# Three slots of 65024-byte rows with half-row loads, full-row late stores and 4096-column instructions, in an element-wise kernel limited by its transfers

## The chip, the cores and the metric

The kernel runs on one core of a Trainium2 chip. The metric is the device time of one execution in microseconds (us), as a median of several runs. The profile shows compute engines (ACT, DVE, POOL) and 16 DMA engines, which moved 536.98 MB in the kernel before, nearly all of it its input and output, between HBM, the main memory, and the on-chip memory SBUF. PSUM is another on-chip memory. All runs compared here are fast, with a granted clock of 1.0, unless the text says otherwise.

## The reference

The kernel computes the inverse complementary error function of 8192 x 8192 floats. That is 268 MB in and 268 MB out, and every element stands alone.

```python
def setup_inputs():
    return {"x": np.clip(np.random.randn(8192, 8192).astype(np.float32) * 0.3 + 1.0, 0.01, 1.99)}

def reference(x):
    return special.erfcinv(x).astype(np.float32)
```

Both kernels approximate it by `(ln(1 - (x-1)^2) + KAPPA) * (B*x - B)`. Nothing in the argument depends on that formula.

## The kernel before

The input is cut into tiles: 128 partitions, each with one contiguous row of 12288 floats (49152 bytes). Four buffers turn round. The SP queue issues loads, and the ACT queue issues stores. A load into a buffer waits until the store that last read this buffer has landed. Each tile is loaded by one DMA and stored by one DMA, both in full rows.

```python
_FULL = 12288
_HEAD = (2048, 6144)
_TAIL = (6144, 4096, 2048)

_CHUNK = 2048
_BUFS = 4

_LEAD = 49152

# ... (pools, constants)
    io = ctx.enter_context(tc.tile_pool(name="io", bufs=_BUFS))
    psum = ctx.enter_context(
        tc.tile_pool(name="ps", bufs=2, space=bass.MemoryType.PSUM)
    )

    def flat(ap, i):
        return ap[P * starts[i] : P * starts[i + 1]].rearrange("(p w) -> p w", p=P)

    views = []
    room = 0

    def load():
        nonlocal room, buf
        i = len(views)
        w = widths[i]
        if w > room:
            buf, room = io.tile([P, _FULL], fp32, name="xt"), _FULL
        v = buf[:, _FULL - room : _FULL - room + w]
        room -= w
        views.append(v)
        nc.sync.dma_start(out=v, in_=flat(xf, i))

    buf = None

    def compute(i):
        step = min(_CHUNK, widths[i] // 2)
        for c in range(0, widths[i], step):
            d = views[i][:, c : c + step]
            ps = psum.tile([P, _CHUNK], fp32, name="ps")
            s = ps[:, 0:step]
            nc.scalar.activation(
                out=s, in_=d, func=mybir.ActivationFunctionType.Square,
                bias=neg_one, scale=1.0,
            )
            nc.scalar.activation(
                out=s, in_=s, func=mybir.ActivationFunctionType.Ln,
                bias=pos_one, scale=-1.0,
            )
            nc.gpsimd.tensor_scalar(
                out=d, in0=d, scalar1=float(_B), scalar2=float(-_B),
                op0=mult, op1=add,
            )
            nc.vector.scalar_tensor_tensor(
                out=d, in0=s, scalar=float(_KAPPA), in1=d, op0=add, op1=mult
            )

    ctx.enter_context(tc.manual_schedule())
    for i in range(n):
        while len(views) < n and starts[len(views) + 1] - starts[i] <= _LEAD:
            load()
        compute(i)
        nc.scalar.dma_start(out=flat(of, i), in_=views[i])
```

Cuts: the imports, the constants and the launch.

Of the kernel before, what the change touches and what calls it, by code (L numbers as in the profile page):

```python
# [1 line left out]

# [4 lines left out]


_B = 0.24401313
_KAPPA = -3.62385604  # L10



_FULL = 12288
_HEAD = (2048, 6144)
_TAIL = (6144, 4096, 2048)

_CHUNK = 2048
_BUFS = 4

_LEAD = 49152


@with_exitstack
def kernel(
    ctx: ExitStack,
    tc: tile.TileContext,
    x: bass.AP,
    out: bass.AP,
):  # L30
    nc = tc.nc
    P = nc.NUM_PARTITIONS
    fp32 = mybir.dt.float32
    mult = mybir.AluOpType.mult
    add = mybir.AluOpType.add

    xf = x.rearrange("r c -> (r c)")
    of = out.rearrange("r c -> (r c)")
    cols = x.shape[0] * x.shape[1] // P
    n_full, rest = divmod(cols - sum(_HEAD) - sum(_TAIL), _FULL)  # L40
    assert rest == 0
    widths = list(_HEAD) + [_FULL] * n_full + list(_TAIL)
    n = len(widths)
    starts = [0]
    for w in widths:
        starts.append(starts[-1] + w)

    consts = ctx.enter_context(tc.tile_pool(name="consts", bufs=1))
    neg_one = consts.tile([P, 1], fp32)
    nc.vector.memset(neg_one, -1.0)  # L50
    pos_one = consts.tile([P, 1], fp32)
    nc.vector.memset(pos_one, 1.0)  # L52

    io = ctx.enter_context(tc.tile_pool(name="io", bufs=_BUFS))
    psum = ctx.enter_context(
        tc.tile_pool(name="ps", bufs=2, space=bass.MemoryType.PSUM)
    )

    def flat(ap, i):
        return ap[P * starts[i] : P * starts[i + 1]].rearrange("(p w) -> p w", p=P)  # L60

    views = []
    room = 0

    def load():
        nonlocal room, buf
        i = len(views)
        w = widths[i]
        if w > room:
            buf, room = io.tile([P, _FULL], fp32, name="xt"), _FULL  # L70
        v = buf[:, _FULL - room : _FULL - room + w]
        room -= w
        views.append(v)
        nc.sync.dma_start(out=v, in_=flat(xf, i))  # L74

    buf = None

    def compute(i):
        step = min(_CHUNK, widths[i] // 2)
        for c in range(0, widths[i], step):  # L80
            d = views[i][:, c : c + step]
            ps = psum.tile([P, _CHUNK], fp32, name="ps")
            s = ps[:, 0:step]
            nc.scalar.activation(  # L84
                out=s, in_=d, func=mybir.ActivationFunctionType.Square,
                bias=neg_one, scale=1.0,
            )
            nc.scalar.activation(  # L88
                out=s, in_=s, func=mybir.ActivationFunctionType.Ln,
                bias=pos_one, scale=-1.0,  # L90
            )
            nc.gpsimd.tensor_scalar(  # L92
                out=d, in0=d, scalar1=float(_B), scalar2=float(-_B),
                op0=mult, op1=add,
            )
            nc.vector.scalar_tensor_tensor(  # L96
                out=d, in0=s, scalar=float(_KAPPA), in1=d, op0=add, op1=mult
            )

    ctx.enter_context(tc.manual_schedule())  # L100
    for i in range(n):
        while len(views) < n and starts[len(views) + 1] - starts[i] <= _LEAD:
            load()
        compute(i)
        nc.scalar.dma_start(out=flat(of, i), in_=views[i])  # L105


# [1 line left out]
_INS = ['x']  # L109
_OUTS = [((8192, 8192), 'float32')]  # L110


# [23 lines left out]
```

## Time and profile before

| what | value |
|---|---|
| median of 3 runs | 1249.54 us (1247.71 to 1253.46) |
| span of the profiled run | 1245.9 us |
| bytes moved | 536.98 MB at 431 GB/s |
| busy: ACT, DVE, POOL | 79%, 47%, 39% |

These lines are from the page of the kernel before. The line DMA is the busy share of the 16 DMA engines in 40 equal slices of the span, in tenths; GB/s is what they moved. q1 is the load queue, q10 the store queue. The line after those gives the shares of the chain of work that ended last. The last two give the DMA issues: count, size of each, and the median time from issue to landing.

```profile
span 1245.9 us, 1637 instructions
DMA  9999999999999999999999999999999999999998
GB/s 393 431 432 437 439 432 431 429 436 439 436 431 429 436 431 443 429 431 431 437 441 431 431 431 437 429 440 431 433 432 434 441 431 431 431 437 434 431 429 371
DMA packets 13261, 536.98 MB, mean 431 GB/s; under 512 B 1472, under 2 KB 1472, under 8 KB 1472
q1 hardware_dynamic: 6624, 268.44, 49.9%
q10 hardware_dynamic: 6624, 268.44, 49.8%
...
DMA 74%; ACT 22%; DVE 3%; issue 0%; another core or an unknown queue 0%; SPq 0%; ACTq 0%; DVEq 0%
...
xt<-in_x_dram SPq DMA_DIRECT2D x41, 6144.0 KB, 45.9
out_dram<-xt ACTq DMA_DIRECT2D x41, 6144.0 KB, 44.5
```

From the view of waits: who waited for whom, the total in us, how often, and the longest wait. The first line is ACT waiting for loaded data, the second the load queue waiting for a buffer.

```profile
ACT ps L84 <- DMA xt<-in_x_dram: 224.4, 40, 6.7
```

```profile
SPq L74 <- DMA out_dram<-xt: 1145.7, 40, 33.1
```

From the groups of instructions with shapes kept apart (busy us, mean ns of one | idle before it and its releaser), the two sizes of one ACTIVATE.

```profile
L84 ACT ACTIVATE ps<-xt,neg_one 128x2048 f32<-128x2048 f32 x254 | 499.1, 1965 | 232.8 <-DMA xt<-in_x_dram 219.8 <-DVE xt L96 13.0
...
L84 ACT ACTIVATE ps<-xt,neg_one 128x1024 f32<-128x1024 f32 x4 | 4.5, 1114 | 4.6 <-DMA xt<-in_x_dram 4.6
```

From the table by stretches (stretch, length, busy time of DVE, ACT and POOL, clock, DMA share, GB/s): nearly the whole run, and a piece from its middle.

```profile
2.00:1236.00 1234.00, 584.60 (x256) 984.47 (x516) 484.86 (x256) 1.00 1.00 433
500.00:620.00 120.00, 57.50 (x26) 96.28 (x51) 47.52 (x25) 1.00 1.00 433
```

The trace also has one record for each DMA packet, with start, duration and size. One row is one packet (41 DMAs of 128 rows are 5248 packets of 49152 bytes in each queue), and each DMA ends in 16 more packets of 4 bytes (1472 for 92 DMAs, about 9 ns each). The records of this kernel give 611 ns for 16384 bytes, 912 for 24576 and 1815 for 49152. So a packet takes 36.74 ns per 1000 bytes and about 9 ns more: 27.2 GB/s per engine, 435 GB/s for 16.

### The profile page before, as it was taken

How to read it: one execution, taken by the hardware profiler on the slowest of the kernel's cores; microseconds unless marked ns; L12 is line 12 of the kernel's file. 1: busy time of each engine (PE TensorE's matmuls, PEld its weight loads, DVE VectorE, ACT ScalarE, POOL GpSimd, SP SyncE). 2: the span in 40 equal slices, each digit the busy share in tenths (PEclk: the TensorE clock that was granted, in tenths of full speed). 3: DMA queues.
4: the chain of work that ended last, by engine and by line, in shares of the span. 5: the costliest groups of instructions: out<-in, count | busy, mean ns of one | idle time of the engine just before them, and what ended most of it. 6: DMA issues, size and time to landing. Idle time of an engine off the chain costs nothing.

```text
span 1245.9 us, 1637 instructions
## 1 busy us (share of the span) xinstructions
DVE 587.1 (47%) x260; ACT 987.7 (79%) x518; POOL 487.2 (39%) x262
## 2 busy tenths in 40 slices
DVE  3555545444444444444454444544444444444453
ACT  6999887778887788888877788888888878777895
POOL 2444443333433344343433334343343434333342
DMA  9999999999999999999999999999999999999998
GB/s 393 431 432 437 439 432 431 429 436 439 436 431 429 436 431 443 429 431 431 437 441 431 431 431 437 429 440 431 433 432 434 441 431 431 431 437 434 431 429 371
DMA packets 13261, 536.98 MB, mean 431 GB/s; under 512 B 1472, under 2 KB 1472, under 8 KB 1472
## 3 DMA queue, kind: packets, MB, share of 16 engines
q1 hardware_dynamic: 6624, 268.44, 49.9%
q10 hardware_dynamic: 6624, 268.44, 49.8%
q14 instruction: 13, 0.11, 0.0%
HBM read 268.44 MB, written 268.44 MB: 431 GB/s over the span
## 4 chain that ended last, share of the span: by engine, by line
DMA 74%; ACT 22%; DVE 3%; issue 0%; another core or an unknown queue 0%; SPq 0%; ACTq 0%; DVEq 0%
DMA xt<-in_x_dram 39%; DMA out_dram<-xt 35%; ACT ps L88 11%; ACT ps L84 11%; DVE xt L96 3%; SPq L74 0%; ACTq L105 0%; DVEq L96 0%
## 5 line engine op out<-in xcount | busy, mean ns | idle before, releaser
L96 DVE SCALAR_TENSOR_TENSOR xt<-ps,xt 128x2048 f32<-128x2048 f32 (+1 forms) x258 | 587.0, 2275 | 652.6 <-POOL xt L92 642.9
L92 POOL TENSOR_SCALAR xt<-xt 128x2048 f32<-128x2048 f32 (+1 forms) x258 | 487.0, 1887 | 751.8 <-ACT ps L84 749.9
L84 ACT ACTIVATE ps<-xt,neg_one 128x2048 f32<-128x2048 f32 (+1 forms) x258 | 503.6, 1952 | 237.5 <-DMA xt<-in_x_dram 224.4
L88 ACT ACTIVATE ps<-ps,pos_one 128x2048 f32<-128x2048 f32 (+1 forms) x258 | 497.6, 1929 | 8.4
L84 ACT ACT_TABLE_LOAD x1 | 1.3, 1283 | 5.7 <-DMA xt<-in_x_dram 5.7
L88 ACT ACT_TABLE_LOAD x1 | 1.3, 1283 | 0.0
L50 DVE MEMSET neg_one<- 128x1 f32 x1 | 0.1, 59 | 0.8 <-PEq L120 0.8
L120 POOL MEMSET const-float32-0.0<- 128x1 f32 x1 | 0.1, 99 | 0.2 <-issue 0.2
L120 POOL MEMSET const-bfloat16-1.0<- 128x1 bf16 x1 | 0.1, 102 | 0.0
L120 POOL MEMSET const-uint8-127<- 128x1 uint8 x1 | 0.1, 102 | 0.0
L120 POOL MEMSET const-float32-1.0<- 128x1 f32 x1 | 0.1, 99 | 0.0
L52 DVE MEMSET pos_one<- 128x1 f32 x1 | 0.1, 59 | 0.0
## 6 DMA issues: line engine op xcount, KB each, us to landing
xt<-in_x_dram SPq DMA_DIRECT2D x41, 6144.0 KB, 45.9
out_dram<-xt ACTq DMA_DIRECT2D x41, 6144.0 KB, 44.5
xt<-in_x_dram SPq DMA_DIRECT2D x2, 3072.0 KB, 25.4
out_dram<-xt ACTq DMA_DIRECT2D x2, 3072.0 KB, 23.1
xt<-in_x_dram SPq DMA_DIRECT2D x2, 1024.0 KB, 37.4
out_dram<-xt ACTq DMA_DIRECT2D x2, 1024.0 KB, 13.3
xt<-in_x_dram SPq DMA_DIRECT2D x1, 2048.0 KB, 58.0
out_dram<-xt ACTq DMA_DIRECT2D x1, 2048.0 KB, 9.8
```

The source lines that it names most:

```text
L50: nc.vector.memset(neg_one, -1.0)
L52: nc.vector.memset(pos_one, 1.0)
L84: nc.scalar.activation(out=s, in_=d, func=mybir.ActivationFunctionType.Square, bias=neg_one, scale=1.0,)
L88: nc.scalar.activation(out=s, in_=s, func=mybir.ActivationFunctionType.Ln, bias=pos_one, scale=-1.0,)
L92: nc.gpsimd.tensor_scalar(out=d, in0=d, scalar1=float(_B), scalar2=float(-_B), op0=mult, op1=add,)
L96: nc.vector.scalar_tensor_tensor(out=d, in0=s, scalar=float(_KAPPA), in1=d, op0=add, op1=mult)
L120: nc = _bacc.Bacc("TRN2", target_bir_lowering=False, num_devices=1)
```

## The change

The intent is to use longer rows and longer instructions. Three slots of 16256 columns (65024 bytes) take the place of four of 12288. A slot is loaded in two half rows (8192 and 8064 columns) so that computing can start early, and stored in one full row. The store is issued one pair of ACT instructions late, so that ACT never waits for DVE before it issues. Instructions have up to 4096 columns; their intermediate results alternate between PSUM and an SBUF buffer. The ends of the run are cut differently. The core of the diff:

```diff
-_FULL = 12288
-_HEAD = (2048, 6144)
-_TAIL = (6144, 4096, 2048)
 
-_CHUNK = 2048
-_BUFS = 4
+_SLOT = 16256
+_BUFS = 3
 
-_LEAD = 49152
+
+_FULL = ((8192, 8064), (4032, 4096, 4032, 4096), ((16256, 1),))
+
+_HEAD = ((2048, 6144, 4032), (1024, 1024, 2048, 4032, 4096), ((8128, 1), (4096, 1)))
+
+_LAST = (
+    (_FULL[0], _FULL[1], ((16256, 4),)),
+    _FULL,
+    ((4096, 4032), (2048, 2048, 2048, 1008, 976), ((6144, 1), (1984, 1))),
+)
 # ... cut: sums of the slots ...
+    temp = ctx.enter_context(tc.tile_pool(name="temp", bufs=1))
+    temps = ((psum, 4096), (temp, 4032))
 # ... cut: compute() is the same four instructions, into temps in turn ...
     def load():
+        i = len(bufs)
+        b = io.tile([P, _SLOT], fp32, name="xt")
+        bufs.append(b)
+        a = 0
+        for w in slots[i][0]:
+            nc.sync.dma_start(out=b[:, a : a + w], in_=rows(xf, i)[:, a : a + w])
+            a += w
 # ...
+    def store(i, a, w, pieces):
+        nc.scalar.dma_start(
+            out=rows(of, i)[:, a : a + w], in_=bufs[i][:, a : a + w],
+            max_dma_last_dim=None if pieces == 1 else w * 4 // pieces,
+        )
 # ...
+    def issue():
+        while due:
+            i, a, w, pieces = due.pop(0)
+            store(i, a, w, pieces)
+            if a + w == sum(slots[i][0]) and len(bufs) < n:
+                load()
+
     for i in range(n):
-        while len(views) < n and starts[len(views) + 1] - starts[i] <= _LEAD:
-            load()
-        compute(i)
-        nc.scalar.dma_start(out=flat(of, i), in_=views[i])
+        loads, chunks, stores = slots[i]
+        a = done = k = 0
+        for c in chunks:
+            compute(bufs[i][:, a : a + c])
+            issue()
+            a += c
+            while k < len(stores) and done + stores[k][0] <= a:
+                due.append((i, done) + stores[k])
+                done += stores[k][0]
+                k += 1
+    issue()
```

A slot is written as `(loads, instruction widths, stores)`, and a store as `(columns, packets per row)`.

More of the change, by code (lines that the diff above doesn't have):

```diff
@@ L39 @@
     cols = x.shape[0] * x.shape[1] // P
-    n_full, rest = divmod(cols - sum(_HEAD) - sum(_TAIL), _FULL)
+    ends = sum(sum(s[0]) for s in (_HEAD,) + _LAST)
+    n_full, rest = divmod(cols - ends, sum(_FULL[0]))
     assert rest == 0
-    widths = list(_HEAD) + [_FULL] * n_full + list(_TAIL)
-    n = len(widths)
-    starts = [0]
-    for w in widths:
-        starts.append(starts[-1] + w)
+    slots = [_HEAD] + [_FULL] * n_full + list(_LAST)
+    n = len(slots)
+    base = [0]
+    for loads, chunks, stores in slots:
+        w = sum(loads)
+        assert w == sum(chunks) == sum(s for s, _ in stores) and w <= _SLOT
+        base.append(base[-1] + w)
     consts = ctx.enter_context(tc.tile_pool(name="consts", bufs=1))
@@ L55 @@
     psum = ctx.enter_context(
-        tc.tile_pool(name="ps", bufs=2, space=bass.MemoryType.PSUM)
+        tc.tile_pool(name="ps", bufs=1, space=bass.MemoryType.PSUM)
     )
-    def flat(ap, i):
-        return ap[P * starts[i] : P * starts[i + 1]].rearrange("(p w) -> p w", p=P)
-    views = []
-    room = 0
-    def load():
-        nonlocal room, buf
-        i = len(views)
-        w = widths[i]
-        if w > room:
-            buf, room = io.tile([P, _FULL], fp32, name="xt"), _FULL
-        v = buf[:, _FULL - room : _FULL - room + w]
-        room -= w
-        views.append(v)
-        nc.sync.dma_start(out=v, in_=flat(xf, i))
@@ L76 @@
-    buf = None
-    def compute(i):
-        step = min(_CHUNK, widths[i] // 2)
-        for c in range(0, widths[i], step):
-            d = views[i][:, c : c + step]
-            ps = psum.tile([P, _CHUNK], fp32, name="ps")
-            s = ps[:, 0:step]
-            nc.scalar.activation(
-                out=s, in_=d, func=mybir.ActivationFunctionType.Square,
-                bias=neg_one, scale=1.0,
-            )
-            nc.scalar.activation(
-                out=s, in_=s, func=mybir.ActivationFunctionType.Ln,
-                bias=pos_one, scale=-1.0,
-            )
-            nc.gpsimd.tensor_scalar(
-                out=d, in0=d, scalar1=float(_B), scalar2=float(-_B),
-                op0=mult, op1=add,
-            )
-            nc.vector.scalar_tensor_tensor(
-                out=d, in0=s, scalar=float(_KAPPA), in1=d, op0=add, op1=mult
-            )
@@ L100, with rows @@
-    ctx.enter_context(tc.manual_schedule())
-    for i in range(n):
-        while len(views) < n and starts[len(views) + 1] - starts[i] <= _LEAD:
-            load()
-        compute(i)
-        nc.scalar.dma_start(out=flat(of, i), in_=views[i])
+    temp = ctx.enter_context(tc.tile_pool(name="temp", bufs=1))
+    temps = ((psum, 4096), (temp, 4032))
+    def rows(ap, i):
+        return ap[P * base[i] : P * base[i + 1]].rearrange("(p w) -> p w", p=P)
+    bufs = []
+    def load():
+        i = len(bufs)
[5 more added lines that the diff above has]
+            a += w
@@ new lines, with compute @@
+    turn = 0
+    def compute(d):
+        nonlocal turn
+        pool, most = temps[turn]
+        turn = 1 - turn
+        s = pool.tile([P, most], fp32, name="t")[:, 0 : d.shape[-1]]
+        nc.scalar.activation(
+            out=s, in_=d, func=mybir.ActivationFunctionType.Square,
+            bias=neg_one, scale=1.0,
+        )
+        nc.scalar.activation(
+            out=s, in_=s, func=mybir.ActivationFunctionType.Ln,
+            bias=pos_one, scale=-1.0,
+        )
+        nc.gpsimd.tensor_scalar(
+            out=d, in0=d, scalar1=float(_B), scalar2=float(-_B),
+            op0=mult, op1=add,
+        )
+        nc.vector.scalar_tensor_tensor(
+            out=d, in0=s, scalar=float(_KAPPA), in1=d, op0=add, op1=mult
+        )
@@ new lines, in store @@
+    def store(i, a, w, pieces):
+        nc.scalar.dma_start(
+            out=rows(of, i)[:, a : a + w], in_=bufs[i][:, a : a + w],
+            max_dma_last_dim=None if pieces == 1 else w * 4 // pieces,
+        )
+    ctx.enter_context(tc.manual_schedule())
+    for _ in range(min(_BUFS, n)):
+        load()
+    due = []
+    def issue():
[3 more added lines that the diff above has]
+            if a + w == sum(slots[i][0]) and len(bufs) < n:
+                load()
```

## The prediction

> **What bounds the kernel now.** The 16 DMA engines, without a gap. The page gives 536.98 MB at 431 GB/s over a span of 1245.9 us; the two queues' packets fill 49.9% + 49.8% of it. The table by stretches shows 433 GB/s from 2 to 1236 us. ACT, the busiest compute engine, is busy 79% and waits 224.4 us for loads (view of waits). The chain of waits is 74% DMA.
>
> The trace's packet records show that one row is one packet: 16384 bytes take 611 ns, 24576 take 912, 49152 take 1815. That is 36.74 ns per 1000 bytes (27.2 GB/s per engine) plus about 9 ns per packet. Sixteen such engines make 435 GB/s. [...] So bytes alone cost 536.87 MB / 435.5 GB/s = 1232.8 us, and the change moves the same bytes.
>
> **What the change does, costed.**
> 1. Packets. Before: 736 per engine x 9 ns = 6.6 us. After: stores have fewer, longer rows, but loads are halved: a slot has 24 packets per engine for 16256 columns, where 12288 columns had 16. I count 840 per engine: +104 x 9 ns = +0.9 us. Ten more DMAs add 0.1 us.
> 2. Compute. By shapes, an ACTIVATE is about 0.26 us + 0.831 ns per column (1024: 1114 ns, 2048: 1965), so 4096 columns should take 3.67 us; ACT falls from 988 to about 930 us. Off the path: a slot needs 29.3 us of ACT and 38.4 us of DMA.
> 3. Buffers: 3 x 65024 bytes for 4 x 49152. A slot's turn lasts 3 x 38.4 = 115 us. Alone it needs about 70 us (half load 9.6, compute 29.3, late issue 7.3, store 19.2[...]): ample slack.
> 4. Arbitration. [...] With 65024-byte store packets against 32 KB load packets, stores should get two thirds while both have work; loads then are the backlog that keeps the engines busy. This moves waiting, not throughput.
> 5. Late store issue: ACT loses its wait of about 2.8 us per tile before each store; off the path. Risk: the store also waits for the next slot's first half. If loads have drained by then, a store's completion leaves the engines empty[...] before the next load arrives.
> 6. Ends. The first packet comes at 1.7 us in both. Before, about 2.0 us of engine time is lost between 1238 and 1242 us, waiting for the last tile's compute. After, the last full slot's store (19 us) should cover it: -1 to -2 us.
>
> **Sum.** +1.0 (packets) - 1.5 (tail) + about 1 (bubbles; 0 to 0.3 us per slot): -0.5 to +1 us. I predict 1249 us, range 1243 to 1258. Chances: faster by over 2% 1%, within 2% 95%, slower 4%.
>
> **What would show it.** DMA share full between 2 and about 1243 us; 65024-byte packets at about 2398 ns; 32768-byte ones at 1213; stores landing in about 29 us; ACT busy about 930 us yet the span unchanged; ACT's wait for loads about 300 us.
>
> **What would make it wrong.** Bubbles at each store's completion: 31 slots x 1 us are already 2.5%. Or 65024-byte rows moving slower than 27.2 GB/s. [...]bytes alone leave 1.3%.

Five passages of it are cut, because no trace or run of this case shows what they say. The forecast's sum of -0.5 to +1 us keeps all its terms. The sum of about 70 us in item 3 had one more term; the four that stand come to 65.4 us. In item 4 the two thirds are the estimate from the packet lengths. The 1.3% at the end compares 1232.8 us, the bytes at the records' speed, with the measured 1249.5; that bytes can't move faster was not shown.

## The result, and the profile after

| | before | after |
|---|---|---|
| median of 6 runs | 1249.67 us | 1305.1 us (1297.98 to 1308.16) |
| ratio, 95% interval | | 1.0435 (1.0405 to 1.0465) |
| span of the profiled run | 1245.9 us | 1303.2 us |
| ACT busy | 987.7 us | 941.2 us |

A ratio is the mean time of one kernel's fast runs over that of the other's of the same rounds, so it is not quite the ratio of the medians quoted here. The change is 4.4% slower. ACT works less, as it was meant to.

The page of the changed kernel, the same lines as before:

```profile
span 1303.2 us, 1020 instructions
DMA  9999999999999999999999999999999999999998
GB/s 400 430 430 431 418 402 409 418 410 414 392 411 415 398 374 407 420 430 372 408 423 427 423 436 426 392 435 418 414 424 395 410 431 429 406 402 416 420 402 361
DMA packets 15080, 536.94 MB, mean 412 GB/s; under 512 B 1632, under 2 KB 1632, under 8 KB 1760
q1 hardware_dynamic: 9648, 268.44, 50.2%
q10 hardware_dynamic: 5424, 268.44, 48.6%
...
DMA 86%; ACT 8%; issue 2%; DVE 1%; POOL 1%; another core or an unknown queue 0%; ACTq 0%; SPq 0%; DVEq 0%; POOLq 0%
...
out_dram<-xt ACTq DMA_DIRECT2D x31, 8128.0 KB, 35.0
xt<-in_x_dram SPq DMA_DIRECT2D x31, 4096.0 KB, 40.9
xt<-in_x_dram SPq DMA_DIRECT2D x31, 4032.0 KB, 56.1
```

The DMA line is as full as before, yet GB/s falls from about 432 to between 372 and 436 in the middle slices. So the engines are busy and yet move less. A store now lands in 35.0 us, while the second half of a load takes 56.1 us. The loads and stores no longer take equally long.

Its waits:

```profile
ACT t L91 <- DMA xt<-in_x_dram: 327.8, 54, 13.2
```

```profile
SPq L81 <- DMA out_dram<-xt: 1202.4, 31, 47.8
```

Its table by stretches. The share is still 0.98 and 1.00, but 0.98 of 435 GB/s would be 426, and it moved 408; at share 1.00 it moved 417. A full busy share is not full speed.

```profile
500.00:620.00 120.00, 49.24 (x13) 83.60 (x25) 46.90 (x12) 1.00 0.98 408
620.00:740.00 120.00, 53.30 (x13) 87.66 (x25) 46.90 (x12) 1.00 1.00 417
```

Groups of instructions with shapes kept apart. ACT's 4096 columns take 3659 ns, as predicted. POOL's 4096-column instruction takes 4271 ns and its 4032-column one 3551.

```profile
L99 POOL TENSOR_SCALAR xt<-xt 128x4096 f32<-128x4096 f32 x63 | 269.1, 4271 | 233.2 <-ACT t L91 229.5 <-DMA xt<-in_x_dram 3.7
L91 ACT ACTIVATE t<-xt,neg_one 128x4096 f32<-128x4096 f32 x63 | 230.5, 3659 | 0.0
...
L99 POOL TENSOR_SCALAR xt<-xt 128x4032 f32<-128x4032 f32 x63 | 223.7, 3551 | 520.7 <-ACT t L91 520.7
```

The longer one is the one that meets a DVE instruction with both inputs in SBUF (the intermediate result of the pair before lies there). At 500.10 us the POOL instruction starts 0.80 us before the DVE instruction ends; all 63 overlap one, by 0.80 to 1.21 us, and they take on average 0.66 us more than the shorter one's time scaled to its width (3607 ns). The 24 shorter ones that overlap a DVE instruction with one input in PSUM take 3552 ns, as long as the 39 that overlap none (3551). What holds the longer ones up is not shown. This costs little here: POOL is 1% of the chain.

From the chain of the changed kernel (start, length, what), pieces that lie in or reach into 470 to 605 us; pieces of under 0.1 us are left out. One round is a store, then a half-row load that waited for it, then one ACT instruction, which releases the next late store. From store to store it is 83.4 us long (434.65 to 518.06). As 31 full stores fill the run, this round carries two slots, 41.7 us each, where the prediction has 38.4.

```profile
434.65 39.30 DMA out_dram<-xt
474.01 40.27 DMA xt<-in_x_dram
514.37 3.66 ACT t L91
518.06 34.59 DMA out_dram<-xt
552.70 44.02 DMA xt<-in_x_dram
```

**Where the 57.3 us of the two spans come from.** These quantities are worked out from the packet records. "Bytes and packets" is 36.74 ns per 1000 bytes plus 9 ns per packet, summed over all data packets and divided by 16. "Slow packets" is what the durations have beyond that, divided by 16. "Idle" is the engines' time without any data packet, divided by 16; "mid-run" leaves out the first 5 us and the last 10 us before the last packet.

| us | before | after | difference |
|---|---|---|---|
| bytes and packets | 1239.5 | 1240.5 | +1.0 |
| slow packets, loads | 1.8 | 32.5 | +30.7 |
| slow packets, stores | 0.2 | 13.3 | +13.1 |
| idle, mid-run | 0.5 | 13.1 | +12.6 |
| idle, both ends | 4.6 | 5.1 | +0.5 |
| sum | 1246.6 | 1304.5 | +57.9 |

Some packets overlap in the records, so the sums are not exactly the spans (1304.5 against 1303.2 us). Three quarters of the loss are packets that took longer than their bytes need. The usual 65024-byte packet takes 2399 ns and the usual 32768-byte one 1213, as predicted; the means are 2453 and 1315, because some take much longer (the longest 3816 and 2876).

What the slow packets look like, from the records of 32768-byte load packets (start in us: duration in ns), a selection. At 597.9 us most engines begin a new slot's load together, just after the store before it has landed. A store joins at about 605 us:

```
597.93: 1634   597.94: 1728   597.95: 1916   597.95: 1916   597.98: 1785   598.04: 1634
599.57: 1211   599.67: 1211   599.67: 1211   599.74: 1211   599.76: 1211   599.86: 1211
603.57: 2411   603.76: 2234   603.77: 2385   603.80: 2234   603.80: 2375   603.82: 2441
```

In this selection packets are slow when the engines start together (1634 to 1916 ns), then take the usual time (1211), and are slow again just before the first store packets (2234 to 2441). One more quantity shows how often such places come. A queue "stands still" when no engine has a packet of it, counted in gaps over 0.5 us, without the first 20 us and the last 15. Before, the store queue stands still for 39 us of the run and the load queue for 16. After, it is 304 and 92 us. Packet by packet, 22.5 of the 32.5 us of slow loads belong to packets that touch the time from 3.5 us before to 1.5 us after the store queue moves again; the 47 such places are 18% of the span. The slow stores are not there (0.3 of 13.3 us): they are spread over the time in which both queues run, and nothing here explains them.

### The profile page after: what moved, and what is told of

It reads as the page before. It is cut to its first block, busy times and chain, and to the rows that moved or that the text cites. A ratio compares the mean times of both kernels' runs of the same rounds, so it can differ in the third digit from the quotient of the medians.

```text
span 1303.2 us, 1020 instructions
## 1 busy us (share of the span) xinstructions
DVE 567.3 (44%) x136; ACT 941.2 (72%) x270; POOL 505.9 (39%) x138
## 4 chain that ended last, share of the span: by engine, by line
DMA 86%; ACT 8%; issue 2%; DVE 1%; POOL 1%; another core or an unknown queue 0%; ACTq 0%; SPq 0%; DVEq 0%; POOLq 0%
DMA xt<-in_x_dram 48%; DMA out_dram<-xt 38%; ACT t L91 7%; ACT t L95 1%; DVE xt L103 1%; POOL xt L99 1%; SPq L81 0%; ACTq L108 0%; ACTq L91 0%; DVEq L103 0%; POOLq L99 0%
## 5 line engine op out<-in xcount | busy, mean ns | idle before, releaser
L103 DVE SCALAR_TENSOR_TENSOR xt<-t,xt 128x4032 f32<-128x4032 f32 (+4 forms) x134 | 567.2, 4234 | 714.7 <-ACT t L95 488.3
L99 POOL TENSOR_SCALAR xt<-xt 128x4032 f32<-128x4032 f32 (+4 forms) x134 | 505.7, 3774 | 775.4 <-ACT t L91 771.7
L91 ACT ACTIVATE t<-xt,neg_one 128x4032 f32<-128x4032 f32 (+4 forms) x134 | 473.1, 3530 | 330.2 <-DMA xt<-in_x_dram 327.8
L95 ACT ACTIVATE t<-t,pos_one 128x4032 f32<-128x4032 f32 (+4 forms) x134 | 472.4, 3525 | 4.3
L91 ACT ACT_TABLE_LOAD x1 | 1.3, 1283 | 5.8 <-DMA xt<-in_x_dram 5.8
L95 ACT ACT_TABLE_LOAD x1 | 1.3, 1283 | 0.0
## 6 DMA issues: line engine op xcount, KB each, us to landing
xt<-in_x_dram SPq DMA_DIRECT2D x31, 4096.0 KB, 40.9
xt<-in_x_dram SPq DMA_DIRECT2D x31, 4032.0 KB, 56.1
```

The costliest lines, as they stand in the source:

```text
L91: nc.scalar.activation(out=s, in_=d, func=mybir.ActivationFunctionType.Square, bias=neg_one, scale=1.0,)
L95: nc.scalar.activation(out=s, in_=s, func=mybir.ActivationFunctionType.Ln, bias=pos_one, scale=-1.0,)
L99: nc.gpsimd.tensor_scalar(out=d, in0=d, scalar1=float(_B), scalar2=float(-_B), op0=mult, op1=add,)
L103: nc.vector.scalar_tensor_tensor(out=d, in0=s, scalar=float(_KAPPA), in1=d, op0=add, op1=mult)
```

## The experiments

The theories at the start, conjectures to be tested:

- **P (pitch):** sixteen engines walk rows 65024 bytes apart, and these addresses collide in HBM.
- **B (backlog):** with three large slots one computes, one loads and one is stored, so a queue often has no work; the engines then stop and start together.
- **H:** half rows are slow to read. **L:** late store or long instructions cost. **A:** packets of unequal length make one queue run ahead of the other.

Seventeen kernels ran (the numbers e6 and f3 were not used). Those that compute gave correct results; m1 to m4 are transfers only and give wrong results. Times are medians; the ratio is to the kernel before on the same chip. The runs were made on several chips, where the median of the kernel before was 1248.1 to 1250.9 us, so a gap of a few us between two runs of the table is no finding. At a limit of 2% f1 and f4 count as unclear, as their 95% intervals (1.0136 to 1.0226 and 1.0179 to 1.0268) straddle it; both are clearly above 1. m1 to m4 ran once each, which leaves their state unknown.

| run | slots | loads per slot, packet | store packet | late | median us | ratio |
|---|---|---|---|---|---|---|
| after | 3 x 16256 | 2, half row | full row | yes | 1305.1 | 1.0435 |
| e1 | 3 x 15360 | 2, half | full | yes | 1301.5 | 1.0429 |
| e2 | 3 x 16256 | 2, half | full | no | 1325.0 | 1.0591 |
| e3 | 3 x 16256 | 1, full | full | yes | 1383.7 | 1.1068 |
| e4 | 3 x 16256, kernel before | 1, full | full | no | 1283.0 | 1.0243 |
| e5 | 4 x 12288 | 2, half | full | yes | 1299.3 | 1.0400 |
| e7 | 6 x 8128 | 1, full | full | yes | 1248.5 | 1.0000 |
| e8 | 3 x 16256 | 2, half | half | yes | 1284.4 | 1.0286 |
| f1 | 4 x 12288 | 2, half | half | yes | 1272.6 | 1.0181 |
| f2 | 4 x 12288 | 1, full | full | yes | 1248.0 | 0.9973 |
| f4 | 6 x 8128 | 2, half | full | yes | 1280.1 | 1.0224 |
| f5 | 4 x 12288 | 1, full | half | yes | 1288.3 | 1.0334 |
| f6 | 6 x 8128, addresses of after | 1, half of a 65024-byte row | the same | yes | 1248.6 | 1.0002 |
| f7 | 4 x 12288 | 1, half | half | yes | 1249.8 | 1.0004 |

The same quantities as above, in us, for the profiled run of each (e4's profile is left out):

| run | span | bytes and packets | slow loads | slow stores | idle mid-run | store queue still | load queue still |
|---|---|---|---|---|---|---|---|
| before | 1245.9 | 1239.5 | 1.8 | 0.2 | 0.5 | 39 | 16 |
| after | 1303.2 | 1240.5 | 32.5 | 13.3 | 13.1 | 304 | 92 |
| e1 | 1300.2 | 1240.9 | 30.2 | 10.5 | 14.4 | 332 | 170 |
| e2 | 1320.6 | 1240.5 | 28.0 | 21.4 | 29.9 | 300 | 103 |
| e3 | 1382.2 | 1238.2 | 55.6 | 0.4 | 86.6 | 387 | 331 |
| e5 | 1297.4 | 1242.6 | 27.0 | 15.7 | 7.7 | 270 | 27 |
| e7 | 1246.7 | 1242.5 | 1.9 | 0.3 | 0.7 | 49 | 49 |
| e8 | 1285.8 | 1242.6 | 7.9 | 18.3 | 13.0 | 74 | 56 |
| f1 | 1265.6 | 1245.5 | 5.3 | 4.0 | 6.6 | 49 | 15 |
| f2 | 1245.9 | 1239.7 | 1.8 | 0.3 | 0.4 | 30 | 37 |
| f4 | 1276.9 | 1247.0 | 19.3 | 7.9 | 4.5 | 274 | 7 |
| f5 | 1282.0 | 1242.5 | 25.3 | 1.2 | 3.9 | 36 | 245 |
| f6 | 1247.0 | 1242.5 | 1.8 | 0.4 | 0.7 | 52 | 52 |
| f7 | 1247.9 | 1245.5 | 1.7 | 0.0 | 0.4 | 14 | 0 |

### e1: another row length

```diff
-_SLOT = 16256
+_SLOT = 15360
-_FULL = ((8192, 8064), (4032, 4096, 4032, 4096), ((16256, 1),))
+_FULL = ((7680, 7680), (3840, 3840, 3840, 3840), ((15360, 1),))
 # the first slot and the packets of one store near the end are fitted
```

> The changed kernel with only the row length altered: 15360 columns (61440 bytes) per slot row instead of 16256 (65024 bytes); same three slots, half-row loads, late store. Theory P (address pitch: packets are slow because sixteen engines walk rows 65024 bytes apart[...]): extra packet time falls from 46 us to under 8 us, the idle time of 13 us in mid-run stays, so about 1265 us. Theory B (bursts: slow packets come from load-only bursts after the engines ran dry, whatever the pitch): extra packet time stays at 35 to 55 us, about 1300 us.

Measured: 1301.5 us, slow packets 40.7 us in place of 45.8. The pitch of 65024 bytes is not the cause; theory P fell here, and m1 and f6 confirm it.

### e2: the store at once

```diff
             compute(bufs[i][:, a : a + c])
-            issue()
             a += c
             while k < len(stores) and done + stores[k][0] <= a:
                 due.append((i, done) + stores[k])
                 done += stores[k][0]
                 k += 1
-    issue()
+            issue()
```

> The changed kernel with each store issued right after its own slot's last instruction pair, not one pair late. Theory B: loads and stores overlap more, the engines no longer run dry, so both the idle time (13 us in mid-run) and the slow packets (46 us) shrink, to about 1255 to 1275 us. Theory P: the idle time shrinks by up to 10 us, the slow packets stay above 30 us, about 1290 to 1300 us.

Measured: 1325.0 us, slower than the change, with 29.9 us idle. Neither theory expected that. With half-row loads the late store is not what hurts; with three slots it even helps. (With full-row loads it is the other way round: e3, late, takes 1383.7 us and e4, at once, 1275 to 1283 in its fast runs, though these two differ in instruction widths too.) In e2 ACT waits 129.4 us for DVE, against 2.3 in the change, so the waits that the late store was to save are back. Why that leaves the engines idle longer I did not settle.

### e3: full-row loads in three slots

```diff
-_FULL = ((8192, 8064), (4032, 4096, 4032, 4096), ((16256, 1),))
+_FULL = ((16256,), (4032, 4096, 4032, 4096), ((16256, 1),))
```

> The changed kernel with one full-row load per slot instead of two half-row loads. Theory H (half rows: a 32 KB piece of every 65024-byte row makes the reads slow): load packets reach 2398 ns, time about 1260 us or lower. Theories P and B: load packets stay slow (extra time over 20 us); time 1290 to 1320 us, as compute of a slot now starts only when the whole slot has landed.

Measured: 1383.7 us, far outside what all theories expected. Its page and its waits:

```profile
DMA  9999999999999899899989998999989999989989
GB/s 401 428 407 388 373 380 395 414 367 369 386 392 420 363 391 380 373 422 378 373 363 391 422 390 363 373 406 395 390 363 388 395 412 371 388 365 391 418 359 397
```

```profile
ACT t L91 <- DMA xt<-in_x_dram: 412.8, 31, 15.1
```

A late store waits for ACT's first instruction on the next slot, and this waits until that whole slot has landed. With three slots, loading and storing then take turns: the load queue stands still for 331 us and the store queue for 387. ACT waits 412.8 us for loads. The half-row loads of the change soften this, but do not remove it. So theory H fell: full rows make it worse with three slots.

### e4: the kernel before with three 65024-byte slots

```diff
-_FULL = 12288
+_FULL = 16256
-_TAIL = (6144, 4096, 2048)
+_TAIL = (6144, 4096, 1920)
-_BUFS = 4
+_STEP = 2032
+_BUFS = 3
-_LEAD = 49152
+_LEAD = 48768
-        step = min(_CHUNK, widths[i] // 2)
+        step = min(_STEP if widths[i] == _FULL else _CHUNK, widths[i] // 2)
```

> The kernel before with rows of 16256 columns in three buffers instead of 12288 in four: full-row loads, stores at once, 2032-column instructions. Theory P: slow packets as in the changed kernel, 25 us or more of extra packet time, time at least 1275 us. Theory B: with loads and stores overlapping all the time, under 10 us of extra packet time, and a time within 10 us of 1250 plus whatever the engines stand idle.

Measured: its fast runs give 1.0243 of the kernel before (1275.0 to 1283.0 us); two of five runs (1304.4 and 1329.1) were slow, the profiled one among them, so the theories' packet times stay unchecked here. The granted clock was 1.0 in all five, so this spread may be the kernel's own; that was not settled. Same bytes of buffer, same order of work, same short instructions, equal packets: three slots of 16256 in place of four of 12288 cost 2.4% by themselves in the fast runs.

### e5: four slots

```diff
-_SLOT = 16256
-_BUFS = 3
+_SLOT = 12288
+_BUFS = 4
-_FULL = ((8192, 8064), (4032, 4096, 4032, 4096), ((16256, 1),))
+_FULL = ((6144, 6144), (3072, 3072, 3072, 3072), ((12288, 1),))
 # the first slot and the last are fitted
```

> The changed kernel with four slots of 12288 columns in place of three of 16256 (3072-column instructions), everything else kept: half-row loads, full-row late store, stores with twice the bytes per packet. Theory B (backlog: with three slots one computes, one loads and one is stored, so each queue runs out of work or works alone, and engines then start together and slow each other): the load queue keeps a backlog again, idle time under 3 us in mid-run, extra packet time under 10 us, total 1245 to 1262 us. Rival L (late store, half loads or large instructions are what costs): stays at 1285 us or more.

Measured: 1299.3 us. Theory B alone fell: the idle time shrank to 7.7 us, but 42.7 us of slow packets stayed, and the store queue stood still for 270 us. Rival L's forecast was met here; e7 and f1 sort its parts. From its page, the issues and their time to landing:

```profile
xt<-in_x_dram SPq DMA_DIRECT2D x83, 3072.0 KB, 62.4
out_dram<-xt ACTq DMA_DIRECT2D x41, 6144.0 KB, 28.1
```

A store lands in 28.1 us and a half load takes 62.4. The stores run ahead of the loads.

### e7: six slots of half the size

```diff
-_SLOT = 16256
-_BUFS = 3
+_SLOT = 8128
+_BUFS = 6
-_FULL = ((8192, 8064), (4032, 4096, 4032, 4096), ((16256, 1),))
+_FULL = ((8128,), (4096, 4032), ((8128, 1),))
 # the first slot and the last are fitted
```

> The changed kernel with six slots of 8128 columns, the same bytes of buffer and the same 4096- and 4032-column instructions and late store; one full-row load of 32512 bytes and one full-row store per slot. Theory B: buffers come free in smaller pieces, both queues keep a backlog: idle under 3 us, extra packet time under 10 us, total 1246 to 1262 us (packet count alone costs 2 to 3 us). Rival L: 1285 us or more.

Measured: 1248.5 us, the time of the kernel before. It keeps the changed kernel's instructions (up to 4096 columns, PSUM and SBUF in turn), its late store and its buffer bytes. So rival L fell for these: with six slots none of the three costs time. The half-row loads, which L named for e5 as well, are not in e7; f1 and f7 take them up. Its GB/s and issues:

```profile
GB/s 401 429 433 434 432 429 432 433 434 434 434 434 433 434 434 434 433 433 434 432 430 433 434 432 434 434 434 432 431 433 433 434 434 434 434 434 434 433 430 376
...
out_dram<-xt ACTq DMA_DIRECT2D x64, 4064.0 KB, 34.7
xt<-in_x_dram SPq DMA_DIRECT2D x63, 4064.0 KB, 57.4
```

### e8: store packets as short as load packets

```diff
-_FULL = ((8192, 8064), (4032, 4096, 4032, 4096), ((16256, 1),))
+_FULL = ((8192, 8064), (4032, 4096, 4032, 4096), ((16256, 2),))
```

> The changed kernel with each store's rows cut into two packets of 32512 bytes, so that loads and stores have packets of equal size. Rival A (arbitration by packet lets the stores take two thirds and starves the loads): 1255 to 1275 us. Theory B: the slots still turn as before, idle and slow packets remain, within 15 us of 1303.

Measured: 1284.4 us, 21 us below the change, between what the two theories expected: both have a part. The store queue stands still for 74 us in place of 304. Loads are slowed by 7.9 us in place of 32.5, but stores by 18.3 in place of 13.3, and the idle time stays at 13.0 us.

### f2: four slots, full-row loads

```diff
 # against e5
-_FULL = ((6144, 6144), (3072, 3072, 3072, 3072), ((12288, 1),))
+_FULL = ((12288,), (3072, 3072, 3072, 3072), ((12288, 1),))
```

> The four-slot variant (e5, 1299 us) with one full-row load per slot, so that loads and stores both have packets of 49152 bytes; late store and 3072-column instructions stay. Theory A: 1245 to 1260 us. Rival L (the late store costs by itself, most of all with full-row loads): 1275 us or more.

Measured: 1248.0 us. One line takes e5 from 1.0400 to 0.9973. Against e3 the only differences are four slots of 12288 for three of 16256 and the instruction widths that follow: 1248 against 1384 us. Its GB/s and issues, to be compared with e5's:

```profile
GB/s 404 428 430 429 441 431 440 431 429 434 432 442 434 429 429 437 431 442 432 428 437 431 439 434 431 432 436 437 434 431 429 439 429 442 431 429 436 427 428 373
```

```profile
xt<-in_x_dram SPq DMA_DIRECT2D x41, 6144.0 KB, 37.5
out_dram<-xt ACTq DMA_DIRECT2D x41, 6144.0 KB, 46.5
```

### f5: the ratio turned round

```diff
 # against f2: store rows cut into two packets
-_FULL = ((12288,), (3072, 3072, 3072, 3072), ((12288, 1),))
+_FULL = ((12288,), (3072, 3072, 3072, 3072), ((12288, 2),))
```

> The four-slot variant with full-row loads (f2, 1248 us) and each store's rows cut into two packets, so that load packets are twice as long as store packets: the ratio of the changed kernel turned round. Packet count adds 3 us. If only the stores' larger share hurts, because they then land early and leave the store queue empty: 1249 to 1256 us. If any unequal share hurts alike: 1270 us or more.

Measured: 1288.3 us. A cut of the store rows, with the same DMAs in the same order, costs 40 us. Now the loads run ahead and stand still for 245 us:

```profile
xt<-in_x_dram SPq DMA_DIRECT2D x41, 6144.0 KB, 27.4
out_dram<-xt ACTq DMA_DIRECT2D x41, 6144.0 KB, 59.0
```

Against f2 a load lands in 27.4 us in place of 37.5 and a store in 59.0 in place of 46.5. Longer load packets cost 40 us here; longer store packets cost 27 us beside two loads per slot (e5 against f1, below).

### f1 and f7: equal packets, two loads or one

```diff
 # f1, against e5
-_FULL = ((6144, 6144), (3072, 3072, 3072, 3072), ((12288, 1),))
+_FULL = ((6144, 6144), (3072, 3072, 3072, 3072), ((12288, 2),))
 # f7, against f1: one load, its rows cut into two packets
-_FULL = ((6144, 6144), (3072, 3072, 3072, 3072), ((12288, 2),))
+_FULL = ((12288,), (3072, 3072, 3072, 3072), ((12288, 2),))
-            nc.sync.dma_start(out=b[:, a : a + w], in_=rows(xf, i)[:, a : a + w])
+            nc.sync.dma_start(
+                out=b[:, a : a + w], in_=rows(xf, i)[:, a : a + w],
+                max_dma_last_dim=w * 2 if w == 12288 else None,
+            )
```

> The four-slot variant (e5, 1299 us) with each store's rows cut into two packets of 24576 bytes, the size of the load packets. Theory A (packets of unequal size are the main cost once slots are fine enough: stores take two thirds, land early, the store queue then stands empty and loads run alone until all engines switch at once): 1246 to 1262 us, extra packet time under 10 us, load time without any store beside it falls from 270 us to under 80 us. If the packet ratio is only half of it, about 1275 us.

> The four-slot variant with one load and one store per slot, the rows of both cut into two packets of 24576 bytes (f1's packets, f2's DMAs). Against f2 the packet count alone adds 43 x 16 x 9 ns = 6 us, so about 1254 us. If the two separate half-row loads are what leaves f1 at 1272 us: 1252 to 1258 us here. If shorter packets are: 1265 us or more.

Measured: f1 1272.6 us, f7 1249.8. Equal packets take 27 us off e5 (theory A's case of half the loss), but two separate half-row loads still cost 23 us over one load with the very same packets. The length of a packet as such cost only its 9 ns here: f7 has 5.8 us more of bytes and packets than f2, and 1.7 us of slow packets against 2.1. In f1, 9.3 us are slow packets and 6.6 idle in mid-run; why two loads per slot do that, beside one store, was not settled.

### f4: six slots with half-row loads

```diff
 # against e7
-_FULL = ((8128,), (4096, 4032), ((8128, 1),))
+_FULL = ((4096, 4032), (4096, 4032), ((8128, 1),))
```

> The six-slot variant (e7, 1248.5 us) with each load cut into two half-row loads of 16384 and 16128 bytes against store packets of 32512. Packet count alone adds about 65 x 8 x 9 ns = 5 us. Theory A: the two-to-one packets bring back load-only stretches (over 150 us of load time without a store) and 15 us or more of extra packet time, 1270 us or more. Theory B alone (only the size of the slots matters): 1250 to 1258 us.

Measured: 1280.1 us against e7's 1248.5, of which the packet count explains 4.5 (1247.0 less 1242.5). So the half-row loads hurt with small slots too: the store queue stands still for 274 us. This edit changes two things, the ratio of the packets and the number of loads per slot; f1 against f7 shows that the second can cost time by itself, so the 32 us are not those of the ratio alone. The median store lands in 19.4 us, where e7 has 34.7:

```profile
out_dram<-xt ACTq DMA_DIRECT2D x64, 4064.0 KB, 19.4
```

### f6: the addresses of the change

```diff
 # against e7: two slots share rows of 65024 bytes in HBM
-        return ap[P * base[i] : P * base[i + 1]].rearrange("(p w) -> p w", p=P)
+        if i == n - 1:
+            return ap[P * base[i] : P * base[i + 1]].rearrange("(p w) -> p w", p=P)
+        m = i - i % 2
+        both = ap[P * base[m] : P * base[m + 2]].rearrange("(p w) -> p w", p=P)
+        return both[:, (i % 2) * _SLOT : (i % 2 + 1) * _SLOT]
```

> The six-slot variant (e7, 1248.5 us) with two slots sharing rows of 65024 bytes in HBM, each slot one half of every row: the addresses of the changed kernel, with equal packets and buffers freed in small pieces. If half rows of 65024-byte rows are slow in themselves: 1255 us or more, extra packet time over 8 us. If not: within 4 us of e7.

Measured: 1248.6 us, slow packets 2.2 us. Rows 65024 bytes apart, read and written in halves, were as fast here as e7's (1248.5 us, slow packets 2.2). P and H are closed.

### m1: loads alone

Loads only, 24 bursts of six shapes, each into the same buffer and so started after the one before has landed; then two streams over three buffers.

```diff
+    for pitch, w in ((12288, 12288), (16256, 16256), (16256, 8128), (15360, 15360), (12288, 6144), (8128, 8128)):
+        for _ in range(4):
+            load(bufs[0], pitch, (w,))
+    for pitch, pieces in ((16256, (8192, 8064)), (12288, (12288,))):
+        for k in range(6):
+            load(bufs[k % 3], pitch, pieces)
```

> Wrong result on purpose: loads only, no computing. 24 bursts, each started after the one before has landed, with rows 49152, 65024 and 61440 bytes apart, full or half; then two streams with two or three loads always queued. Theory B with synchronised starts: packets of every burst run slow (speed 0.75 to 0.95 of 27.2 GB/s per engine) in all pitches alike, while the streams run at 0.98 or more. Theory P (pitch): bursts of 65024 are slow, those of 49152 fast. If all bursts run at full speed, slow packets need stores or computing beside them and both theories lack their cause.

Measured: every burst has 0.6 to 0.9 us of slow packets, whatever its shape, in its first packets; the later ones take no longer than their bytes need. About 1.3 us pass between the last packet of a burst and the first of the next. After its first DMA, a stream loses at most 0.04 us per DMA. From its table by stretches, two stretches of bursts (rows of 49152 bytes, then of 65024) and the two streams:

```profile
18.00:72.00 54.00, 0.00 (x0) 1.00 0.85 350
72.00:160.00 88.00, 0.00 (x0) 1.00 0.90 378
400.00:500.00 100.00, 0.00 (x0) 1.00 1.01 435
500.00:558.00 58.00, 0.00 (x0) 1.00 0.99 429
```

From start to start a burst takes 2.5 to 3.3 us longer than its bytes and packets need: the 1.3 us, the slow packets, and engines that end before the last one does. That is what a start from empty cost here, and it is much the same for all pitches.

### m2: both queues always full

Stores from one buffer and loads into two others, in five stretches; each stretch starts with the loads and is joined by the stores some us later.

```diff
+    for row, pieces, cut, n_loads, n_stores in (
+        (12288, (12288,), 1, 6, 6),
+        (12288, (6144, 6144), 1, 4, 8),
+        (16256, (8128, 8128), 1, 3, 6),
+        (16256, (8128, 8128), 2, 5, 5),
+        (8128, (8128,), 1, 8, 8),
+    ):
 # n_stores stores from one buffer, n_loads loads into two, then a load into the stores' buffer
```

> Wrong result on purpose: transfers alone, no computing, both queues always full. Five stretches: packets of 49152 against 49152 bytes, load 24576 against store 49152, 32512 against 65024, 32512 against 32512 cut from 65024-byte rows, 32512 against 32512 in 32512-byte rows. Theory A in the form that an unequal mix is only unfair, not slow in itself: shares of about one third and two thirds in stretches 2 and 3, one half elsewhere, and speeds of 0.99 or more in all five. If the unequal mix is slow in itself: speeds under 0.98 in stretches 2 and 3.

Measured: in stretch 2 one 3.1 MB load lands for each 6.3 MB store, every 21.8 us, so the shares are one to two. Speeds, once both run, are 1.000 in stretches 1, 2 and 5 and mostly 0.98 to 1.00 in 3 and 4, with one load at 0.92 (in stretch 4, whose packets are equal). So the unequal mix of stretch 2 was unfair, not slow in itself. From the table by stretches, pieces of stretch 1 (equal packets) and stretch 2 (one to two):

```profile
50.00:160.00 110.00, 0.00 (x0) 1.00 1.01 436
232.00:385.00 153.00, 0.00 (x0) 1.00 1.00 434
```

But at each of the five places where stores join running loads, the load in flight lost 1.0 to 1.45 us.

### m3 and m4: does a start of the store queue cost time by itself?

A chain of loads that never runs dry. In m3 small stores, in m4 large ones, each start from an empty store queue.

```diff
+    # m3
+    widths = [0] * 8 + [4096] * 10 + [1024] * 10
+    for k, w in enumerate(widths):
+        nc.sync.dma_start(out=bufs[k % 3][:, :], in_=rows(xf, P * 12288 * k, 12288))
+        if w:
+            nc.scalar.dma_start(out=rows(of, put, w), in_=bufs[k % 3][:, 0:w])
+    # m4: 42 loads into four buffers, the first 21 in full rows, the rest in halves;
+    # after every third, a store of its whole slot in full rows
```

> Wrong result on purpose: transfers alone. 28 full-row loads of 49152-byte rows in a chain that never runs dry; beside the last 20 of them a small store each (10 of 16384-byte rows, 10 of 4096-byte rows), which always starts from an empty store queue. Theory R (a restart of the store queue slows the loads in flight by itself): about 1 us of extra load packet time per store, 10 us or more over the first ten. If the restarts are harmless: under 0.2 us per store.

> Wrong result on purpose: transfers alone. 42 loads of 49152-byte rows in a chain, the first 21 in full rows and the rest in halves; every third has its slot stored in full rows, so that 14 large stores each start from an empty store queue beside running loads. If a large store's start slows loads by itself: 0.7 us or more of extra load packet time per start, 10 us or more in all. If the slow packets need something else (an irregular pattern, engines restarting from idle): under 4 us in all.

Measured: in m3 the first store costs the loads 0.5 us and the other 19 nothing. In m4 the first store costs 1.26 us, the next five, beside full-row loads, at most 0.03 each. Beside half-row loads each store has 0.1 to 0.3 us of slow packets of its own and its neighbour loads up to 0.4. In all the loads of m4 have 3.9 us of slow packets, of which 0.8 are the very first load's and 1.3 the first store's start. So a start from an empty queue was not costly by itself in these runs, and theory R (a restart of the store queue slows the loads) fell. What the costly places in m1, m2, m3 and m4 have in common (0.6 to 0.9 us per burst, 1.0 to 1.45 per joining store, 0.5 and 1.26 at the first store) is that the engines had been started together from empty and were disturbed for the first time. Later starts were nearly free in m3 and beside the full rows of m4 (at most 0.03 us each). What makes the difference is not shown.

## Why the prediction was wrong, point by point

- **What bounds the kernel:** right. At the speed of the records the bytes alone cost 1233 us in both kernels: they give 27.2 GB/s per engine, 435 for 16, and full stretches ran at 433 to 436.
- **Packets, +1.0 us:** right. The trace has 840 packets per engine, as counted; at 9 ns each, +1.0 us.
- **Compute:** right in size (ACT 941 us against about 930; 3.66 us for 4096 columns against 3.67) and right that it is off the path: ACT's wait for loads grew to 327.8 us (predicted about 300). POOL's longer instructions beside DVE (4271 ns in place of 3607) were missed; POOL is 1% of the chain.
- **Ends, -1.5 us:** not seen; idle time at both ends went from 4.6 to 5.1 us.
- **Late store:** the risk was named rightly, and e3 shows it at its worst. With four or six slots and equal packets it is free (f2 1248.0 us, e7 1248.5).
- **Bubbles, "about 1 (bubbles; 0 to 0.3 us per slot)":** mis-sized. The idle time in mid-run grew by 12.6 us, 0.4 us per slot. "Ample slack" was the error. Its sum took a half load at 9.6 us and a store at 19.2, each alone on the engines; side by side they took 40.9 and 35.0 us from issue to landing, waits behind other transfers included. With these the same sum (40.9 + 29.3 + 7.3 + 35.0) is 112.5 us of a turn of 115. The idle time follows the slots: it stays at 13.0 us with equal packets (e8) and falls to 7.7 with four slots (e5).
- **Arbitration, "This moves waiting, not throughput":** this is the step that failed. The shares were predicted rightly, and m2 shows them: one 3.1 MB load for each 6.3 MB store. Loads did keep the engines busy, in all but 13.1 us of the mid-run; but busy engines lost throughput. Stores that take two thirds land early (35.0 us against 56.1 for a second half load), and then the store queue stands still: 304 us in place of 39. Each turn the engines go from both queues to one and back, and around these places load packets take longer (22.5 us). The prediction put slow packets at zero; they were +43.8 us, three quarters of the loss.
- **"65024-byte rows moving slower":** named as a danger, and not it: in e1 another length is as slow, in m1 bursts of all lengths cost the same, in m2 store packets of 65024 bytes run at 0.99 or more, and in f6 the same addresses are fast.

What the runs show as causes, each alone enough to slow the kernel: three large slots with equal packets (e4, 2.4%; e3 against f2, 136 us with the late store), and unequal packets (longer loads: f5 against f2, 40 us, by the packets' length alone; longer stores, as in the change: e5 against f1, 27 us, beside two loads per slot). Two loads per slot beside one store cost 23 us even with equal packets (f1 against f7). f4 against e7, 32 us, has the last two together. The parts do not add up: e5 has one more slot than the change and is 6 us faster, which their intervals do not separate (1.0382 to 1.0419 and 1.0405 to 1.0465); e8 has equal packets and gains 21; and only both together, with one load per slot, reach 1248 (f2, e7, f7). Longer stores with one load per slot were not tried. The longer instructions, the late store and the addresses cost nothing with six slots (e7, f6).

Open stays why packets slow down at these places, what slows the stores while both queues run, why two loads per slot hurt with equal packets, and why e2 is slower than the change. No version beat the kernel before: e7, f2, f6 and f7 are all within 0.3% of it, as a kernel at 433 GB/s of 435 would be.

## What to carry to other kernels

Where the DMA engines are the limit, these runs speak for keeping loads and stores alike: the same packet length, one DMA each per slot, and enough slots (four or more here) that both queues always have one waiting. Large DMAs alone did not give full speed: nearly all here are of 2 to 8 MB in the steady part, and yet the kernels moved from 388 GB/s (e3) to 431 (f2). A busy share of 100% does not say that the engines move all they can (1.00 at 417 GB/s in the changed kernel, at 433 in the one before); look at GB/s, and at whether one queue lands much earlier than the other. Cutting a DMA in two to start computing sooner was not free: 23 us even with equal packets (f1 against f7), for a reason that stays open.
